# All weights stored in DRAM in the order of their tiles, one run of 4 or 8 KB per partition and load

## The chip, the cores and the metric

The kernel runs on one core of one Trainium2 chip. The metric is the device time of one execution, in microseconds (us). The core has a matrix engine (PE; its weight loads are listed apart as PEld), a vector engine (DVE), an activation engine (ACT), a general engine (POOL), a sync engine (SP, which here issues nearly all loads) and 16 DMA engines that carry the loads from DRAM into the core's memory of 128 partitions.

## The reference

Two transformer blocks follow each other on 256 tokens of width 1024. The first has two layers; each normalises and modulates the tokens, multiplies them with one wide projection matrix, runs attention, an mLSTM and a gated MLP side by side, and projects back:

```python
for l in range(DEPTH):                                   # block 1, DEPTH = 2
    mod_lat = silu_c @ w_ada[l] + b_ada[l]               # w_ada[l]: 1024 x 3072
    mod_ctx = silu_cc @ w_ada[l] + b_ada[l]
    x, ctx = _layer(x, ctx, mod_lat, mod_ctx, ...)       # w_in[l]: 1024 x 3344, w_out[l]: 1024 x 1024
x = _rms_norm(x, g_final)
for i in range(DEPTH):                                   # block 2
    mod = (ada_in @ w_ada_2[i] + b_ada_2[i]).reshape(b, 6, d)        # 1024 x 6144
    hm = rmsnorm(x, norm_mix[i]) * (1 + sc_m) + sh_m
    y = dilated_mixer(hm, a_w_in, a_w_out, ...) if i == 0 else forgetting_mixer(hm, b_w_in, b_w_out, ...)
    x = x + g_m * y
    hf = rmsnorm(x, norm_ffn[i]) * (1 + sc_f) + sh_f
    x = x + g_f * hierarchical_moe(hf, ..., w_gate[i], w_up[i], w_down[i])   # 16 experts
```

`a_w_in` is 1024 x 9216, `b_w_in` 1024 x 3088. `hierarchical_moe` gives every token two of 16 experts, each `silu(t @ w_gate) * (t @ w_up) @ w_down` with an inner width of 256. All values are float32, about 290 MB of weights in one execution.

## The kernel before, in words

Weights are read once, straight from DRAM, and used at once. Nearly every load goes into a tile called `raw`, 128 partitions x 4 x 512 float32 (1 MB); there are four of them, taken in turn, and a load into one waits until its last reader is done. SP issues the loads in program order, so an issue that waits holds back all later ones.

A projection takes the two halves (512 rows each) of a 1024 x 512 piece of its matrix as two `raw` tiles (`fetch`, L421). Row `k*128 + p` of a half lies in partition `p`, place `k`. ACT makes `wh`, an fp16 copy, DVE makes `wl`, the fp16 rest (L429), and PE multiplies `wh` and `wl` with the fp16 tokens `x`, and `wh` with their rest `y`. Where the 512 columns come from two places of the matrix, `fetch` issues one DMA for each place, and the rows of a DMA are as long as its piece of columns: 2 KB for 512 columns, 1 KB for 256, 64 bytes for the 16 gate columns.

The modulation is a matrix-vector product, straight in float32 on `raw` (`ps_ad<-raw,cz`). That of layer 0 is needed first of all and is done in four quarters (`ada_quarters`, L547): for each quarter two `raw` tiles, each of two DMAs of 512 KB with rows of 1 KB, one for the shift and one for the scale. After the second tile ACT copies the sum to `adasb`, PE transposes it, and DVE forms `mod` and `modA`. The tokens come in `xin` (four tiles, ctx and x); ACT squares each (`sq`), POOL makes the root `rs` in two steps, DVE scales `xin`; PE transposes it, and ACT and DVE form `nv` by `mod` and `modA`, then `x` and `y`, the two operands of the first projection, `kv` (272 columns). The other modulations load rows of 4 or 8 KB (L496).

In the MoE, two experts make a pair. `moe_gu` loads gate and up weights (L1930): every second pair into `raw`, 512 KB in rows of 4 KB for each DMA, the others into `x` tiles, 256 KB in rows of 2 KB. `moe_dn` loads `w_down` in rows of 8 KB, 1 MB in one run. After the first pairs stands a branch (`If`, L2114), for experts with more than 64 tokens; it isn't taken with these inputs, but every engine has to pass it.

The order of the instructions on each engine is set by a scheduler when the kernel is built, which estimates how long each instruction takes, the loads too.

Of the kernel before, what the change touches and what calls it, by code (L numbers as in the profile page):

```python
# [10 lines left out]
F32 = mybir.dt.float32  # L11
# [7 lines left out]
ds = bass.DynSlice  # L19
# [5 lines left out]
D = 1024  # L25
# [84 lines left out]
def quad(v):  # L110

    return np.ascontiguousarray(v.reshape(-1, 128, 4).transpose(1, 0, 2).reshape(128, -1))


# [45 lines left out]
class Stage:  # L160
# [251 lines left out]

    def fetch(self, segs, halves=range(2)):

        raws = []
        for hf in halves:
            raw = self.raw()
            o = 0
            for s in segs:
                n = s.shape[1]  # L420
                self.nc.sync.dma_start(raw[:, :, o:o + n],  # L421
                                       s.rearrange("(k p) n -> p k n", p=128)[:, 4 * hf:4 * hf + 4, :])
                o += n
            raws.append(raw[:, :, :o])
        return raws
# [20 lines left out]

    def load_w(self, segs):

        halves, raws = [], self.fetch(segs)
        self.convq.append((halves, self.conv_steps(raws, halves)))  # L450
        return halves
# [82 lines left out]
    def ada_quarters(self, gname, res):  # L534

        w, z, n = self.ap["w_ada"][0], self.cz, D // 4
        for r in range(2):
# [3 lines left out]
        for h in range(4):  # L541
            p = self.ps("ad")
            for k0 in (0, 4):
                raw = self.raw().rearrange("p a n -> p (a n)").rearrange("p (k j n) -> p k j n", k=4, j=2)
                for j in range(2):
                    src = w[k0 * 128:k0 * 128 + 512, j * D + h * n:j * D + h * n + n]
                    self.nc.sync.dma_start(raw[:, :, j], src.rearrange("(k p) n -> p k n", p=128))  # L547
                for k in range(4):
                    for j in range(2):
                        self.mm(p[32 * j:32 * j + 32, :n], z[:, k0 + k, :], raw[:, k, j], k0 + k == 0, k0 + k == 7,  # L550
                                tile_position=(0, 32 * j))
                if k0 == 0:
                    yield
            sb = self.w1("adasb")
            self.act(sb[:64], p[:64, :n], AF.Copy)
            q = self.ps("tr")
            for b in range(2):
                self.tr(q[:, b * 64:b * 64 + 64], sb[:64, b * 128:b * 128 + 128], 64)
            qv = q[:, :128].rearrange("p (b j r) -> p j b r", b=2, j=2)
            bias = self.P("bada1_0")[:, :16].rearrange("p (j k) -> p j k", j=2)  # L560
            c = slice(2 * h, 2 * h + 2)
            for r, (a, sh, sc) in reversed(list(enumerate(res))):
                self.tt(sc[:, c], qv[:, 1, :, r], bias[:, 1, c], OP.add)
                self.stt(a[:, c], sc[:, c], 1.0, self.P(f"{gname}_0")[:, c], OP.add, OP.mult)
                self.tt(sh[:, c], qv[:, 0, :, r], bias[:, 0, c], OP.add)
            yield
# [176 lines left out]
class Block1(Stage):  # L743
    def layer_w(self, l):

        w, wo = self.ap["w_in"][l], self.ap["w_out"][l]
        at = {"kv": ((1280, 1536), (3328, 3344)), "ckv": ((2304, 2816),), "cq": ((2048, 2304), (2816, 3072)),
              "z": ((3072, 3328), (512, 768)), "q": ((768, 1280),), "gmlp": ((0, 512),), "bz": ((1536, 2048),)}
        return [[w[:, a:b] for a, b in at[n]] for n in SEQ] + [[wo[:, 0:512]], [wo[:, 512:1024]]]

# [521 lines left out]
    def run(self):  # L1272
# [82 lines left out]
        def follow1(T, x):  # L1355
            r = self.rstd2(T)
            for n in range(2):
# [8 lines left out]

        w = self.ap["a_w_in"]
        self.W01 = self.layer(1, xT[1], W, (0, 1, 2, 3), loader(xd), gates1, follow1,
                              [[w[:, n * D:n * D + 512]] for n in range(2)])


class Block2(Block1):
# [220 lines left out]
    def dilated(self, xT):  # L1593
        nc = self.nc
        w = self.ap["a_w_in"]
# [3 lines left out]
        wo = [self.ap["a_w_out"][:, n * 512:(n + 1) * 512] for n in range(2)]  # L1599

        def load(n):
            if n < len(units):
                g, hf, k = units[n]
                c = (g * 3 + k) * D + hf * 512
                W[n] = self.load_w([w[:, c:c + 512]])
            else:
                W[n] = self.load_w([wo[n - len(units)]])

# [80 lines left out]
    def fox(self, xT, norm):  # L1689
        nc = self.nc  # L1690
        w = self.ap["b_w_in"]
        cols = [(k * D + hf * 512, k * D + hf * 512 + 512) for hf in range(2) for k in range(3)]
        W = {}
        wo = [self.ap["b_w_out"][:, n * 512:(n + 1) * 512] for n in range(2)]

        def load(n):
            if n < len(cols):
                W[n] = self.load_w([w[:, cols[n][0]:cols[n][1]]])
            else:
                W[n] = self.load_w([wo[n - len(cols)]])  # L1700
# [4 lines left out]
        nc.sync.dma_start(wr, w[:, 3072:3088].rearrange("(k p) n -> p k n", p=128))  # L1705
        W[0] = self.conv(self.fetch([w[:, cols[0][0]:cols[0][1]]]), 1)
        with self.tc.issue_after(self.tail[0]), self.tc.issue_after(self.tail[1]):
# [56 lines left out]
        for hf in range(2):  # L1764
# [8 lines left out]
            else:  # L1773
# [4 lines left out]
                for T in range(2):  # L1778
# [7 lines left out]
                                          U, lambda hf=hf, U=U: fin(hf, U), (s3[:, hs], NC)))  # L1786
        return [W[len(cols)], W[len(cols) + 1]]

# [129 lines left out]
    def moe_gu(self, i, P, part=range(8)):  # L1918
# [3 lines left out]
        for q in part:  # L1922
            a, k = divmod(2 * q, 8)
            if k % n:
                continue
            t = (self.x4(F32, (2, 512)) if P % 2 else self.raw()).rearrange("p a n -> p (a n)")
            t = t.rearrange("p (m j n) -> p m j n", m=2, j=n)
# [182 lines left out]
    def overflow(self, i, cnt, CAP):  # L2110
# [3 lines left out]
        with tc.If(rv > CAP):  # L2114
# [7 lines left out]
            with tc.For_i(0, 16, 1) as e:  # L2122
                raws = []
                for q in range(4):
                    t = self.wtile(("wh", "wl")[q % 2], (2, 512), F32)
                    for n, nm in enumerate(("w_gate", "w_up")):
                        nc.sync.dma_start(t[:, :, n * 256:n * 256 + 256],
                                          ap[nm][i, ds(e, 1)].rearrange("a (h p j) n -> p (a h) j n", h=2, j=4)[
                                              :, q // 2, q % 2 * 2:q % 2 * 2 + 2, :])
                    raws.append(t)  # L2130
                gc = self.small("gcol", 2)
                nc.vector.tensor_copy(gc[:, :, None], over[:, :, ds(e, 1)])
                hTs = []
                for T in range(2):
                    p = self.ps("tr")
                    for k in range(8):
                        self.mm(p, fT[:, k, T * 128:T * 128 + 128], raws[k // 2][:, k % 2], k == 0, k == 7)
                    t = self.w1("mt")
# [66 lines left out]
```

## Time and profile before

| | |
|---|---|
| median of 3 runs | 1310.13 us (1310.04 to 1313.8) |
| profiled execution | 1307.47 us, of which the span is 1305.5 us |
| PE busy | 1207.0 us, 92% of the span |
| DVE, ACT, POOL busy | 771.4, 628.1, 237.3 us |
| DMA | 292.36 MB, mean 224 GB/s; 114814 packets, 104724 of them under 8 KB |
| SP's hardware queue (q1) | 111972 packets, 60.8% of the 16 DMA engines' time |

The span is the time between the first and the last instruction of the profiled execution. A packet is one row of a transfer. The DMA share of a stretch can come out a little over 1, since packets of an engine overlap at their ends.

### The profile page before, as it was taken

To read this page: it belongs to the slowest core of one execution; us is meant where nothing else is said; L and a number is where in the kernel's file an instruction comes from. 1 tells how busy PE (TensorE), PEld (TensorE's weight loads), DVE (VectorE), ACT (ScalarE), POOL (GpSimd) and SP (SyncE) were. 2 spreads that over 40 slices of the span, in tenths; PEclk is the share of its full clock that TensorE was granted. 3 is DMA by queue.
4 is the path that set the end of the run, shared out by engine and by line. 5 is a ranking of instruction groups with operands and counts; after the bars stand their busy time and mean duration, and the time that the engine had idled before them with its cause. 6 is when DMAs were issued, how large, how long until landed. Compare 5 with 4: busy or idle time off the path is not lost. (4 is left out here: it accounts for less than half of the span.)

```text
span 1305.5 us, 21252 instructions
## 1 busy us (share of the span) xinstructions
PE 1207.0 (92%) x8064; PEld 574.9 (44%) x8064; DVE 771.4 (59%) x1787; ACT 628.1 (48%) x1373; POOL 237.3 (18%) x254
## 2 busy tenths in 40 slices
PE   6889999889999999899999999989997999889987
PEld 2434544444444544344545555445422445545432
DVE  3676645785568667866688767753213587663212
ACT  3535544443545545667677767433113656533111
POOL 1122000121230001251443234010001414010000
PEclk9999999999999999999999999989999899989998
DMA  9853456244384474598544545858898776618895
GB/s 322 284 173 135 163 186 214 94 161 148 135 273 157 139 265 154 185 324 307 167 163 161 194 162 210 299 219 300 342 353 313 269 292 228 227 37 324 329 354 198
DMA packets 114814, 292.36 MB, mean 224 GB/s; under 512 B 10890, under 2 KB 29450, under 8 KB 104724
## 3 DMA queue, kind: packets, MB, share of 16 engines
q1 hardware_dynamic: 111972, 281.57, 60.8%
q0 software_dynamic: 2736, 9.39, 2.3%
q8 instruction: 65, 1.06, 0.3%
q14 instruction: 41, 0.34, 0.1%
HBM read 288.80 MB, written 2.13 MB: 223 GB/s over the span
## 5 line engine op out<-in xcount | busy, mean ns | idle before, releaser
L264 PE MATMUL ps_mm<-wh,x 128*128 128x512 f16 (+1 forms) x1120 | 379.5, 378 | 4.6 <-DVE kn L251 2.0
L264 PEld LDWEIGHTS <-x 128*128 128x128 f16 (+1 forms) x2344 | 189.2, 98 | 245.9 <-issue 91.0
L264 PE MATMUL ps_mm<-wl,x 128*128 128x512 f16 (+1 forms) x736 | 276.0, 375 | 0.0
L429 DVE SCALAR_TENSOR_TENSOR wl<-raw,wh 128x1024 f16<-128x1024 f32 (+2 forms) x188 | 222.8, 1212 | 58.0 <-ACT wh L248 57.5
L248 ACT ACTIVATE wh<-raw 128x1024 f16<-128x1024 f32 (+2 forms) x188 | 182.8, 1015 | 62.5 <-PE ps_mm L264 56.0
L264 PE MATMUL ps_mm<-wh,y 128*128 128x512 f16 (+1 forms) x480 | 173.4, 373 | 0.4 <-DVE y L251 0.3
L264 PE MATMUL ps_ad<-raw,cz 128*32 128x512 f32 (+1 forms) x640 | 112.4, 569 | 11.7 <-DMA raw<-in_w_ada 11.7
L298 POOL TENSOR_SCALAR hss<-hss 128x8 f32<-128x8 f32 (+2 forms) x58 | 20.7, 357 | 444.6 <-DVE hss L697 425.7
L299 POOL TENSOR_TENSOR hr<-hss,nhalf 128x8 f32<-128x8 f32 (+2 forms) x58 | 90.5, 1561 | 4.8
L264 PEld LDWEIGHTS <-y 128*128 128x128 f16 x560 | 53.9, 99 | 60.3 <-issue 12.3
L259 DVE SCALAR_TENSOR_TENSOR oh<-ps_tr,ka,oh 128x512 f16<-128x512 f32 x32 | 24.0, 751 | 86.9 <-ACT oh L248 86.7
L248 ACT ACTIVATE e<-e,ka 128x128 f32<-128x128 f32 (+1 forms) x128 | 56.6, 443 | 24.8 <-DVE ka L1556 24.8
L268 PE MATMUL ps_tr<-consts,e 128*128 128x128 f32 x352 | 59.2, 280 | 1.7 <-ACT e L248 0.5
L264 PE MATMUL ps_mm<-wh,big 128*128 128x512 f16 x192 | 58.1, 379 | 0.2 <-DVE big L259 0.2
L268 PEld LDWEIGHTS ps_tr<-consts,e 128*128 128x128 f32 x352 | 40.8, 141 | 29.3 <-ACT e L248 6.0
L248 ACT ACTIVATE oh<-ps_tr,ka 128x512 f16<-128x512 f32 x32 | 22.0, 687 | 57.5 <-PE ps_tr L264 57.5
L251 DVE TENSOR_TENSOR e2l<-ps_tr,e2h 128x384 f16<-128x384 f32 x64 | 34.1, 553 | 23.4 <-ACT e2h L248 22.5
L248 ACT ACTIVATE e<-ps_s,mx 128x512 f32<-128x512 f32 (+1 forms) x48 | 29.1, 612 | 34.4 <-DVE mx L994 34.4
L251 DVE TENSOR_TENSOR el<-ps_tr,eh 128x512 f16<-128x512 f32 (+1 forms) x48 | 28.1, 597 | 27.2 <-ACT eh L248 27.0
L248 ACT ACTIVATE e2h<-ps_tr 128x384 f16<-128x384 f32 x64 | 30.0, 481 | 26.5 <-PE ps_o L264 14.5
L264 PEld LDWEIGHTS ps_ad<-raw,cz 128*32 128x32 f32 x640 | 21.0, 110 | 48.9 <-issue 27.1
L264 PEld LDWEIGHTS <-big 128*128 128x128 f16 x288 | 28.1, 98 | 32.4 <-DVE big L259 0.3
(377 smaller groups left out, 1988.1 us busy)
## 6 DMA issues: line engine op xcount, KB each, us to landing
raw<-in_w_ada SPq DMA_DIRECT2D x40, 1024.0 KB
raw<-in_a_w_in SPq DMA_DIRECT2D x36, 1024.0 KB
raw<-in_w_ada SPq DMA_DIRECT2D x64, 512.0 KB
raw<-in_w_in SPq DMA_DIRECT2D x16, 1024.0 KB
big<-in_w_down SPq DMA_DIRECT2D x16, 1024.0 KB
qk<-in_w_down SPq DMA_DIRECT2D x16, 1024.0 KB
x<-in_w_gate SPq DMA_DIRECT2D x64, 256.0 KB
x<-in_w_up SPq DMA_DIRECT2D x64, 256.0 KB
```

The costliest lines, as they stand in the source:

```text
L248: return self.nc.scalar.activation(out, in_, func, **kw)
L251: return self.nc.vector.tensor_tensor(out, a, b, op=op)
L259: return self.nc.vector.scalar_tensor_tensor(out, a, s, b, op0=op0, op1=op1)
L264: return self.nc.tensor.matmul(out, lhsT, rhs, start=start, stop=stop, **kw)
L268: return self.nc.tensor.transpose(out, in_, self.C("ident")[:n, :n])
L298: self.nc.gpsimd.tensor_scalar(in_, in_, eps, None, op0=OP.add)
L299: self.nc.gpsimd.tensor_tensor(out, in_, self.nhalf.to_broadcast(list(in_.shape)), op=OP.pow)
L429: (on or self.nc.vector).scalar_tensor_tensor(wl, raw, WS, wh, op0=OP.mult, op1=OP.subtract)
```

## The change

The host stores each weight matrix in the order in which the tiles want it: for each tile all its values of partition 0 (places `k` = 0 to 3 one behind the other), then those of partition 1, and so on. Each load is then one DMA with one run per partition: 8 KB for a `raw` tile, 4 KB for an `x` tile, 4352 bytes for `kv`, 512 bytes for the forget-gate columns `wfr` (before: 64 bytes). Where a tile was filled by two DMAs, one remains: SP has 369 rows in its order before, and 232 now. In a `raw` tile of the MoE the order of gate and up within a partition changes too, and the views follow. `w_down`, the other modulations (L496) and `bias` are as they were; so are the bytes, the tiles, their number, and the work of PE, ACT, DVE and POOL.

```diff
+def blocks(w):
+    return w.reshape(2, 4, 128, -1).transpose(0, 2, 1, 3).reshape(2, 128, -1)
+def weight_arrays(a):
+    w = {}
+    for l in range(2):
+        for n, cs in COLS.items():
+            w[f"w_{n}_{l}"] = blocks(np.concatenate([a["w_in"][l][:, c:d] for c, d in cs], 1))
...
+    v = a["w_ada"][0][:, :2 * D].reshape(2, 4, 128, 2, 4, D // 4)
+    w["w_ada_0"] = v.transpose(4, 0, 2, 1, 3, 5).reshape(4, 2, 128, -1)
+    v = np.stack([a["w_gate_2"], a["w_up_2"]], 2).reshape(2, 16, 2, 2, 128, 2, 2, 256)
+    w["w_gu"] = v.transpose(0, 1, 4, 3, 5, 2, 6, 7).reshape(2, 16, 128, 4096)
+    return w
...
-    def fetch(self, segs, halves=range(2)):
+    def fetch(self, src, halves=range(2)):
         raws = []
         for hf in halves:
-            raw = self.raw()
-            o = 0
-            for s in segs:
-                n = s.shape[1]
-                self.nc.sync.dma_start(raw[:, :, o:o + n],
-                                       s.rearrange("(k p) n -> p k n", p=128)[:, 4 * hf:4 * hf + 4, :])
-                o += n
-            raws.append(raw[:, :, :o])
+            n = src.shape[2]
+            raw = self.raw().rearrange("p k n -> p (k n)")[:, :n]
+            self.nc.sync.dma_start(raw, src[hf])
+            raws.append(raw.rearrange("p (k n) -> p k n", k=4))
         return raws
...
-                raw = self.raw().rearrange("p a n -> p (a n)").rearrange("p (k j n) -> p k j n", k=4, j=2)
-                for j in range(2):
-                    src = w[k0 * 128:k0 * 128 + 512, j * D + h * n:j * D + h * n + n]
-                    self.nc.sync.dma_start(raw[:, :, j], src.rearrange("(k p) n -> p k n", p=128))
+                raw = self.raw().rearrange("p a n -> p (a n)")
+                self.nc.sync.dma_start(raw, w[h, k0 // 4])
+                raw = raw.rearrange("p (k j n) -> p k j n", k=4, j=2)
...
-            for m, nm in enumerate(("w_gate", "w_up")):
-                src = self.ap[nm][i, 2 * P + a].rearrange("(h p j) n -> p h j n", h=2, j=4)
-                self.nc.sync.dma_start(t[:, m], src[:, k // 4, k % 4:k % 4 + n, :])
-            ws[a].extend(t[:, :, j] for j in range(n))
+            self.nc.sync.dma_start(t, self.ap["w_gu"][i, 2 * P + a][:, k * 512:(k + n) * 512])
+            t = t.rearrange("p (q m j n) -> p q m j n", q=n // 2, m=2, j=2)
+            ws[a].extend(t[:, j // 2, :, j % 2] for j in range(n))
```

The callers in block 1, in the two mixers of block 2 and in the branch of the MoE pass the new arrays in the same way.

Since the scheduler sees other loads, it also orders a few instructions otherwise, nearly all of them in the first 75 us. In the listings a row is a line of the kernel, the operation and what it writes and reads; a line number of the helpers is 34 higher after the change (L248 and L282 are the same line). POOL's order is the same in both.

On ACT, at the start of the program, before: the first of the four `xin` tiles is squared before the first `adasb`, three after it, and the second half of the `kv` weights is converted (`wh` with 2x272) after the second `adasb`.

```order
L248 ACTIVATE sq,ss<-xin 128x1024
L248 ACTIVATE adasb<-ps_ad 64x256
L248 ACTIVATE sq,ss<-xin 128x1024 x3
L248 ACTIVATE nv<-ps_tr,mod_103,modA_104 128x256
L248 ACTIVATE x_99<-nv 128x2x256
L248 ACTIVATE adasb<-ps_ad 64x256
L248 ACTIVATE wh<-raw 128x2x272 x2
L248 ACTIVATE nv<-ps_tr,mod_101,modA_102 128x256
```

And the same place after the change:

```order
L282 ACTIVATE sq,ss<-xin 128x1024 x2
L282 ACTIVATE adasb<-ps_ad 64x256
L282 ACTIVATE sq,ss<-xin 128x1024 x2
L282 ACTIVATE nv<-ps_tr,mod_103,modA_104 128x256
L282 ACTIVATE x_99<-nv 128x2x256
L282 ACTIVATE wh<-raw 128x2x272 x2
L282 ACTIVATE adasb<-ps_ad 64x256
L282 ACTIVATE nv<-ps_tr,mod_101,modA_102 128x256
```

One square has moved ahead of the first `adasb`, and the conversion ahead of the second. DVE's counterpart moves with it: the two `wl` rows (L429) of that half stand before the second group of `mod` and `modA` now, and after it before.

On SP, the loads of the first 60 us, before (`xin` are the tokens, `w_in` here the `kv` columns, then `q`):

```order
L547 DMA raw<-in_w_ada 128x4x256 x2
L421 DMA raw<-in_w_in 128x4x256
L421 DMA raw<-in_w_in 128x4x16
L1284 DMA xin<-in_ctx 128x1024
L547 DMA raw<-in_w_ada 128x4x256 x2
L1284 DMA xin<-in_ctx 128x1024
L1284 DMA xin<-in_x 128x1024 x2
L547 DMA raw<-in_w_ada 128x4x256 x4
L421 DMA raw<-in_w_in 128x4x256
L421 DMA raw<-in_w_in 128x4x16
L547 DMA raw<-in_w_ada 128x4x256 x8
L421 DMA raw<-in_w_in 128x4x512 x2
```

After the change:

```order
L575 DMA raw<-in_w_ada 128x2048
L453 DMA raw<-in_w_kv 128x1088
L1310 DMA xin<-in_ctx 128x1024
L575 DMA raw<-in_w_ada 128x2048
L1310 DMA xin<-in_ctx 128x1024
L1310 DMA xin<-in_x 128x1024 x2
L575 DMA raw<-in_w_ada 128x2048 x2
L453 DMA raw<-in_w_kv 128x1088
L575 DMA raw<-in_w_ada 128x2048 x4
L453 DMA raw<-in_w_q 128x2048 x2
```

The tiles are loaded in the same order; each pair of DMAs into one tile has become one.

## Rows read from the trace of the kernel before

**Rows 1.** Stretches: start, length, busy time (count) by engine, PE clock, DMA share, GB/s.

```profile
core 0: us, PE busy (x) PEld busy (x) DVE busy (x) ACT busy (x) POOL busy (x), PEclk, DMA share, GB/s
0.00:30.00 30.00, 18.05 (x98) 7.71 (x98) 9.91 (x34) 11.21 (x21) 5.09 (x15) 0.94 0.99 320
30.00:60.00 30.00, 23.69 (x167) 13.94 (x168) 16.85 (x44) 14.68 (x25) 1.25 (x4) 0.94 0.94 322
60.00:820.00 760.00, 726.04 (x5174) 354.41 (x5176) 527.81 (x1183) 432.25 (x953) 176.06 (x187) 1.00 0.54 185
820.00:1010.00 190.00, 172.98 (x1010) 74.05 (x1009) 71.28 (x193) 53.70 (x127) 10.82 (x9) 0.96 0.84 308
```

**Rows 2.** PE's waits, 0 to 62 us: total us, times, longest.

```profile
PE ps_ad L264 <- DMA raw<-in_w_ada: 8.1, 4, 5.8
PE ps_tr L268 <- DVE xin L255: 2.2, 1, 2.2
```

**Rows 3.** PE's waits, 62 to 820 us.

```profile
PE ps_ad L264 <- DMA raw<-in_w_ada: 3.6, 5, 1.9
```

**Rows 4.** PE's waits over the whole span, the other one for a load.

```profile
PE ps_mm L264 <- DMA raw<-in_w_up: 4.2, 2, 2.2
```

**Rows 5.** DMA from 3 to 36 us: packets, sizes, rate.

```profile
DMA packets 11085, 11.57 MB, mean 351 GB/s; under 512 B 1404, under 2 KB 10559, under 8 KB 11084
```

**Rows 6.** DMA from 17 to 23 us, nearly only rows of 1 KB.

```profile
DMA packets 2103, 2.09 MB, mean 348 GB/s; under 512 B 64, under 2 KB 2103, under 8 KB 2103
```

**Rows 7.** DMA from 38 to 41 us, nearly only rows of 2 KB.

```profile
DMA packets 564, 1.12 MB, mean 374 GB/s; under 512 B 16, under 2 KB 16, under 8 KB 564
```

**Rows 8.** DMA from 966 to 972.6 us, mostly rows of 4 KB.

```profile
DMA packets 756, 2.74 MB, mean 416 GB/s; under 512 B 87, under 2 KB 87, under 8 KB 755
```

**Rows 9.** DMA from 952.6 to 956.6 us, rows of 8 KB (`w_down`).

```profile
DMA packets 224, 1.70 MB, mean 424 GB/s; under 512 B 17, under 2 KB 17, under 8 KB 17
```

**Rows 10.** Instructions in time, start: start us, us, engine, line, operation [idle before <- releaser].

```profile
13.34 1.91 PE L264 MATMUL ps_ad<-raw,cz 128*32 128x256 f32 x14 [0.87 <-DMA raw<-in_w_ada]
15.29 0.38 ACT L248 ACTIVATE adasb<-ps_ad 64x256 f32<-64x256 f32 x1 [3.82 <-PE ps_ad L264]
15.56 1.04 ACT L248 ACTIVATE sq<-xin 128x1024 bf16<-128x1024 f32 x1
...
20.14 0.57 POOL L299 TENSOR_TENSOR rs<-ss,nhalf 128x1 f32<-128x1 f32 x1
...
21.41 0.54 DVE L256 TENSOR_SCALAR nv<-ps_tr,modA,mod 128x256 f32<-128x256 f32 x1
...
22.67 0.29 PE L264 MATMUL ps_mm<-wh,x 128*128 128x272 f16 x1
...
24.66 1.92 PE L264 MATMUL ps_ad<-raw,cz 128*32 128x256 f32 x16
26.62 0.38 ACT L248 ACTIVATE adasb<-ps_ad 64x256 f32<-64x256 f32 x1 [4.01 <-PE ps_ad L264]
26.90 1.19 ACT L248 ACTIVATE wh<-raw 128x544 f16<-128x544 f32 x2
...
28.00 1.36 DVE L429 SCALAR_TENSOR_TENSOR wl<-raw,wh 128x544 f16<-128x544 f32 x2
...
30.53 0.29 PE L264 MATMUL ps_s<-wh,x 128*128 128x272 f16 x1 [0.85 <-ACT x L248]
```

**Rows 11.** The same, 44 to 60 us.

```profile
44.63 1.92 PE L264 MATMUL ps_ad<-raw,cz 128*32 128x256 f32 x16
...
48.45 1.99 ACT L248 ACTIVATE wh<-raw 128x1024 f16<-128x1024 f32 x2
...
59.91 0.39 PE L264 MATMUL ps_mm<-wh,x 128*128 128x512 f16 x1 [2.00 <-DVE kn L251]
```

**Rows 12.** Stretch 52 to 56 us, columns as in rows 1.

```profile
52.00:56.00 4.00, 3.39 (x17) 2.31 (x18) 3.54 (x10) 2.10 (x3) 0.00 (x0) 0.57 1.09 342
```

**Rows 13.** The same as rows 10, behind the branch of the first MoE.

```profile
959.09 0.34 SPq L1930 DMA_DIRECT2D raw<-in_w_gate  x1
959.19 1.17 POOL L620 DMA_DIRECT2D gate<-gs  x2 [90.94 <-PEq L2114]
...
966.03 1.06 PE L264 MATMUL ps_mm<-raw,wh 128*64 128x512 f32 x2 [2.01 <-DMA raw<-in_w_up]
```

**Rows 14.** SP's waits, 948 to 960 us: total us, times, longest.

```profile
SPq L2114 <- SPq L2114: 8.1, 5, 2.5
```

**Rows 15.** Queues that fetch instructions, whole span: packets, MB, share of DMA time.

```profile
q8 instruction: 65, 1.06, 0.3%
q14 instruction: 41, 0.34, 0.1%
```

More of the change, by code (lines that the diff above doesn't have):

```diff
@@ L445, in conv, with load_w @@
         return halves
-    def load_w(self, segs):
-        halves, raws = [], self.fetch(segs)
+    def load_w(self, src):
+        halves, raws = [], self.fetch(src)
         self.convq.append((halves, self.conv_steps(raws, halves)))
@@ L744, in layer_w @@
     def layer_w(self, l):
[L746 to L749, printed above, removed]
+        return [self.ap[f"w_{n}_{l}"] for n in SEQ] + [self.ap[f"w_out_{l}"][n] for n in range(2)]
     def layer(self, l, xT, W, order, load_x, gates, follow, last, first=None):
@@ L1365, in follow1 @@
             self.done.add(("x", T))
-        w = self.ap["a_w_in"]
         self.W01 = self.layer(1, xT[1], W, (0, 1, 2, 3), loader(xd), gates1, follow1,
-                              [[w[:, n * D:n * D + 512]] for n in range(2)])
+                              [self.ap["a_w_in"][n] for n in range(2)])
 class Block2(Block1):
@@ L1598, in dilated @@
         W = {}
-        wo = [self.ap["a_w_out"][:, n * 512:(n + 1) * 512] for n in range(2)]
+        wo = [self.ap["a_w_out"][n] for n in range(2)]
         def load(n):
             if n < len(units):
-                g, hf, k = units[n]
-                c = (g * 3 + k) * D + hf * 512
-                W[n] = self.load_w([w[:, c:c + 512]])
+                W[n] = self.load_w(self.ap["a_w_in"][n])
             else:
-                W[n] = self.load_w([wo[n - len(units)]])
+                W[n] = self.load_w(wo[n - len(units)])
         def merge(hf, g, Us):
@@ L1690, in fox @@
         nc = self.nc
-        w = self.ap["b_w_in"]
-        cols = [(k * D + hf * 512, k * D + hf * 512 + 512) for hf in range(2) for k in range(3)]
         W = {}
-        wo = [self.ap["b_w_out"][:, n * 512:(n + 1) * 512] for n in range(2)]
+        units = [self.ap["b_w_in"][n] for n in range(6)] + [self.ap["b_w_out"][n] for n in range(2)]
         def load(n):
[L1697 to L1700, printed above, removed]
+            W[n] = self.load_w(units[n])
         lf = self.keep("lf", 2, 16)
@@ L1704, in fox @@
         wr = self.w1("wfr", (8, 16))
-        nc.sync.dma_start(wr, w[:, 3072:3088].rearrange("(k p) n -> p k n", p=128))
-        W[0] = self.conv(self.fetch([w[:, cols[0][0]:cols[0][1]]]), 1)
+        nc.sync.dma_start(wr.rearrange("p k n -> p (k n)"), self.ap["b_w_f"])
+        W[0] = self.conv(self.fetch(units[0]), 1)
         with self.tc.issue_after(self.tail[0]), self.tc.issue_after(self.tail[1]):
@@ L2188 @@
         "bias2": dilated_bias(a["rel_bias_2"]),
[L2189 to L2191 removed]
+        "w_down": a["w_down_2"], **weight_arrays(a),
         "w_ada_2": a["w_ada_2"], "b_ada_2": a["b_ada_2"],
     }
[L2194 removed]
+    for n in ("w_ada", "b_ada", "g_final"):
         arrs[n] = a[n]
```

34 lines of the change are left out of this document (19 added, 15 removed).

## The prediction

> **What bounds the kernel now.** I read the stretches first, then PE's list of waits, then the DMA rates, and only then single instructions in the places that these three point to. The stretches [rows 1] show two kernels in one. From 60 to 820 us PE is busy 726 of 760 us and the DMA engines are on average half idle: a faster load changes nothing there except where PE stands still for one. In the first 60 us it is the other way: the DMA share is 0.99 and 0.94, and PE works 18.05 and 23.69 of 30 us each. In the first MoE (820 to 1010 us) both are loaded, PE 172.98 of 190 us and DMA 0.84. The list of waits then says what loads cost PE directly: 8.1 us in the first 62 us [rows 2], 3.6 us up to 820 us [rows 3], and 4.2 us in the two MoEs, once in each [rows 4]. (A wait of 2.2 us for `xin` stands behind the load too, through the chain below [rows 2].) The waits for loads are 15.9 us, the most that faster loads can give by these waits alone; more can only come where a late load delayed ACT or DVE first.
>
> The rates tell how much faster a row gets when it is longer. Where the queue is full, rows of 1 KB moved at 348 GB/s [rows 6], 2 KB at 374 [rows 7], 4 KB at 416 [rows 8], 8 KB at 424 [rows 9]; the last is `w_down`, which before the change already is what all loads become, a tile of 1 MB in one run. So 1 KB to 8 KB takes 18% off a transfer (1 - 348/424), 2 KB 12%, 4 KB 2%. From 3 to 36 us the mean is 351 GB/s, and 10559 of 11085 packets are under 2 KB [rows 5]: the stretch that hangs most on loads has the shortest rows.
>
> The Trainium skill ("DMA: Bandwidth & Descriptors", Specifications) says otherwise: 512 B is enough for line rate, and about 358 GB/s is what the DRAM gives one core. By that, rows of 1 KB at 348 have nothing left to gain. The trace disagrees with it, with 424 GB/s at 8 KB [rows 9]; it is weighed below.
>
> **The change part by part.** *The start.* The first product of the modulation needs its second `raw` tile, on which PE waits until 13.34 us [rows 10]. Ahead of and with it SP has asked for two tiles of 1 MB, 0.56 MB of `kv` weights, and 0.5 MB of tokens, 3.27 MB (in units of 10^6 bytes) with the small constants. At the mean of the stretch, 351 [rows 5], that takes 9.3 us, at 424 7.7 us. The tokens have rows of 4 KB already, so I take 1.4 us: the tile comes at about 11.9 instead of 13.3 us, and `adasb` at 13.9 instead of 15.29.
>
> What follows is a chain of small operations on ACT, POOL and DVE. The last three tiles of tokens are squared from 15.56 on, behind `adasb`; POOL's last root starts at 20.14, DVE's `nv` at 21.41, PE's first `kv` matmul at 22.67 [rows 10]. The new order squares the second tile ahead of `adasb`. Its tokens lie in the queue just behind the tile of the modulation, 0.52 MB or 1.2 us later, at 13.1 us; so this square runs from 13.1 to 14.3, 2.3 us earlier than at 15.56 to 16.6, and `adasb` waits for it by some 0.4 us, which the chain of roots hides. POOL's three roots follow the second square at the same pace, since its order and work are the same. I take 2.1 us: the first `kv` matmul at 20.6 instead of 22.67.
>
> The next step is the second quarter (`ps_ad` at 24.66, `adasb` at 26.62). Behind it ACT converts the second half of the `kv` weights (1.19 us from 26.90) and DVE too (1.36 us from 28.00), before they get to `nv` and `x`; only then PE goes on, at 30.53 [rows 10]. In the new order both conversions stand ahead of `adasb`. ACT and DVE are free then, while PE multiplies (20.6 to 24.5 us), if the load is in: the bytes ahead of it and its own are 7.5 MB, about 20.5 us at 424. So their time leaves the path. Not all of the 1.36 us: PE transposes and ACT works on the other half of `nv` meanwhile, so I take 0.8 us. If the load came later than 24.5 us, `adasb` would wait behind it, and these 0.8 us would become a loss of about 1.2; the 4 us between make that unlikely. Together 2.9 us by 30.53.
>
> From there PE is nearly without a gap up to the last quarter at 44.63 [rows 11] and doesn't wait for a load, and a load can't run further ahead than the four tiles, which PE itself frees. What the loads save here stays hidden. At 48.45 ACT converts two pieces in a row (1.99 us) that the new order takes apart, one of them ahead of `nv`, in a gap of ACT: 0.3 us, by 0 to 0.5. So the start gives 2.9 + 0.3 = 3.2 us, and PE's matmul of 59.91 would start at 56.7.
>
> Its bounds: nothing below 1.4 us, the tile's own, unless a rival below takes it back. Above, if all 33 us of [rows 5] were a wait for data, 11.57 MB would take 27.3 instead of 33 us: 5.7 us.
>
> *The middle, 62 to 820 us.* The rows there are 2 KB or 1 KB for projections, and the modulations (unchanged) lie behind them in the same queue. PE waits 3.6 us in five places, 1.9 us in one of them [rows 3]. There the transfer ahead is one tile of the projection (1.05 MB); 348 to 424 takes it from 3.0 to 2.5 us, and one issue less saves about 0.3 us (0.34 us for one at [rows 13]). I take 0.8 us for all five, 0 to 3.6. Nothing else is on the path: PE is the bound.
>
> *The two MoEs.* Rows of 2 KB become 4 KB and of 4 KB 8 KB. PE waits for them only behind the branch: SP gets to the loads at 959.09, PE starts 6.94 us later, having waited 2.01 us [rows 13]. The first tile is two DMAs (gate, up), one now, so its second half is asked for about 0.35 us earlier; and two transfers that POOL issues at the same time share the DMA engines. I take 0.35 us for each of the two MoEs, 0.7 us (0 to 4.2, rows 4). Its cover: none, PE runs on at once.
>
> *Nothing* for the 137 rows fewer on SP: its issues wait for buffers, not for SP. *Nothing* for `wfr` (512 bytes instead of 64 in each row, 64 KB).
>
> The sum is 3.2 + 0.8 + 0.7 = 4.7 us, off the profiled 1307.47 us. I take the same difference from the median of the runs, 1310.13: **1305.4 us**. About 0.3% (3.9 us) is what a measurement of this kernel can tell from no change, so it would count as faster below 1306.2.
>
> **The rivals.** *Hidden or given back.* The start is a chain of waits between five engines, of which the load is one; if the roots or `adasb` set it, or PE idles later instead, 1.4 us or less remain of 3.2, and the rest may give nothing: 1308.5 to 1310.5. It would also go so if the DMA engines gain nothing by longer rows, or still split them: with the rates unchanged, only the reordering of 0.8 to 1.5 us is left, 1309. For it speaks that PE is 92% busy; against it the four rates [rows 6 to 9]. That the rates stay is what the rule of the Trainium skill cited above would make of this change.
>
> *The start hangs on data throughout.* Then it gives 5.7 us [rows 5], with 1.5 us from the rest 7.2. From 52 to 56 us the clock granted to PE was 0.57 [rows 12], so PE's 3.39 us there would take about 2 at full clock; if this stretch goes too, 1.4 more. 1301.5 to 1303. For it speaks the share of 0.99; against it, that PE runs from 30 to 46 us without waiting for a load.
>
> *Slower: instructions come later.* The engines' instructions are fetched over the same DMA engines, 65 and 41 packets [rows 15]. A fetch that stands behind one row on its engine waits for it: 47 ns for 1 KB (348 GB/s over 16 engines), 88 ns for 2 KB, 309 ns for 8 KB. So each can come 0.22 to 0.26 us later, 106 of them 23 to 28 us if all were waited for. It needs 8.6 us (4.7 to undo and 3.9 beyond), which is some 36 of 106 on the path: 1314 to 1320. Against it: fetching shows as a wait at the branch, where SP waits 8.1 us in five pieces [rows 14], and there the queue is full of `w_down`'s 8 KB rows already, so this doesn't get worse. Elsewhere I see no such wait.
>
> **How the numbers follow.** My forecast (1304 to 1307.5) has a chance of 0.45, hidden or given back 0.27, data throughout 0.20, slower 0.08. Of the first, about four fifths lie below 1306.2: faster 0.20 + 0.36 = 0.56. Same is 0.09 + 0.27 = 0.36, slower 0.08. The range runs from 1300.5 (data throughout, and more of the middle's 3.6 us) to 1311.0 (nothing gained, and the spread of the runs); it leaves out the slower case and the tails.
>
> **What would show it.** From 3 to 36 us a rate above 400 GB/s instead of 351, and only the token tiles' rows under 8 KB. The second tile of the modulation lands at about 11.9 us, the first `kv` matmul starts at 20.6, the matmul of 30.53 at 27.7, that of 59.91 at 56.7. PE's wait for `in_w_ada` falls from 11.7 us (rows 2 and 3) by some 2 to 3, that in the MoEs from 4.2 to about 3.5. I am wrong if the rates don't rise; if they do and 59.91 moves by less than 1.5 us, the start is no chain of loads; if it moves by 3 and the whole doesn't, the gain is lost further on.

## The result

| | before | changed |
|---|---|---|
| median of 5 runs | 1313.11 us (1310.04 to 1313.92) | 1299.76 us (1296.04 to 1302.97) |
| ratio | | 0.9896, 95% interval 0.9874 to 0.9919 |
| profiled execution | 1307.47 us, span 1305.5 | 1301.36 us, span 1299.2 |

The changed kernel is faster by 1.0%, about 13.4 us by the medians, where 4.7 us were forecast and 1300.5 us was the low end of the range. A second set of runs gave 0.9893 (0.9871 to 0.9916). The two profiled executions lie only 6.3 us apart in span. One execution is a poor yardstick here: the timed runs of before scatter from 1302.13 us (granted clock 0.981 over the run) to 1320.5 us (0.966), since the stretches at half clock differ from one execution to the next. One more run of before, 1837 us long at a granted clock of 0.617, is left out of every comparison. So the sums below are made by medians of many runs, and the traces say where.

The page of the changed kernel, its head, PE, and the loads:

```profile
span 1299.2 us, 21044 instructions
PE 1207.5 (93%) x8064; PEld 574.7 (44%) x8064; DVE 772.2 (59%) x1787; ACT 628.1 (48%) x1373; POOL 235.2 (18%) x254
DMA packets 51133, 292.34 MB, mean 225 GB/s; under 512 B 5962, under 2 KB 6218, under 8 KB 24660
q1 hardware_dynamic: 48292, 281.56, 58.7%
```

The bytes are the same and the packets less than half; SP's queue needs 58.7% of the DMA engines' time instead of 60.8%. So the change did what it says, and PE's own work (1207.5 us, 1207.0 before) did not change. PE's waits for loads in the whole span, all in one line (total us, times, longest), which answers to rows 2 to 4:

```profile
PE ps_ad L298 <- DMA raw<-in_w_ada: 13.8, 7, 6.7
```

The wait for `in_w_ada` has not fallen by 2 to 3 us but risen, from 11.7 to 13.8 us (12.4 in a second execution). Part of it is that PE now begins with a tile only when the whole tile has landed: its first product starts at 6.71 us, and before, with half a tile, at 5.82:

```profile
5.82 1.03 PE L264 MATMUL ps_ad<-raw,cz 128*32 128x256 f32 x2 [5.82 <-DMA raw<-in_w_ada]
```

The wait for the MoE's weights, 4.2 us in [rows 4], is not 3.5 as forecast but gone. At the start, DMA from 3 to 36 us (as [rows 5]) and instructions in time (as [rows 10, 11]):

```profile
DMA packets 2171, 12.71 MB, mean 385 GB/s; under 512 B 240, under 2 KB 245, under 8 KB 1013
```

```profile
6.71 3.63 PE L298 MATMUL ps_ad<-raw,cz 128*32 128x256 f32 x16 [6.71 <-DMA raw<-in_w_ada]
...
11.76 3.63 PE L298 MATMUL ps_ad<-raw,cz 128*32 128x256 f32 x16 [1.42 <-DMA raw<-in_w_ada]
...
15.43 0.38 ACT L282 ACTIVATE adasb<-ps_ad 64x256 f32<-64x256 f32 x1 [1.26 <-PE ps_ad L298]
...
21.28 0.29 PE L298 MATMUL ps_mm<-wh,x 128*128 128x272 f16 x1 [1.20 <-ACT x L282]
...
29.08 0.29 PE L298 MATMUL ps_s<-wh,x 128*128 128x272 f16 x1
...
55.19 0.39 PE L298 MATMUL ps_mm<-wh,x 128*128 128x512 f16 x1 [1.74 <-DVE kn L285]
```

The second tile is there at 11.76 us (13.3 before, 11.9 forecast), the first `kv` matmul at 21.28 (22.67 before, 20.6 forecast), the matmul of 59.91 at 55.19 (56.7 forecast). So far the gain is 4.7 us. Behind the first MoE's branch (as [rows 13, 14]):

```profile
949.60 0.80 SPq L1952 DMA_DIRECT2D qk<-in_w_down  x2
...
953.01 1.88 SPq L1944 DMA_DIRECT2D raw<-in_w_gu  x4
...
964.58 1.02 PE L298 MATMUL ps_mm<-raw,wh 128*64 128x512 f32 x2
```

And SP's waits there:

```profile
SPq L2129 <- SPq L2129: 1.3, 2, 0.8
```

SP issues the last loads ahead of the branch at 949.6, as before (948.88), but the first behind it at 953.0 instead of 959.09; its waits at the branch are 1.3 us instead of 8.1 [rows 14], and in the second MoE 1.6 instead of 8.4. PE then finds its weights in place. This is what the prediction didn't have, and the experiments are mostly about it.

### The profile page after: what moved, and what is told of

Read it like the earlier page. It is cut to its first block, busy times and chain, and to the rows that moved or that the text cites. A ratio compares the mean times of both kernels' runs of the same rounds, so it can differ in the third digit from the quotient of the medians.

```text
span 1299.2 us, 21044 instructions
## 1 busy us (share of the span) xinstructions
PE 1207.5 (93%) x8064; PEld 574.7 (44%) x8064; DVE 772.2 (59%) x1787; ACT 628.1 (48%) x1373; POOL 235.2 (18%) x254
## 3 DMA queue, kind: packets, MB, share of 16 engines
q1 hardware_dynamic: 48292, 281.56, 58.7%
## 5 line engine op out<-in xcount | busy, mean ns | idle before, releaser
L282 ACT ACTIVATE wh<-raw 128x1024 f16<-128x1024 f32 (+2 forms) x188 | 183.1, 1015 | 62.6 <-PE ps_mm L298 56.5
L298 PE MATMUL ps_ad<-raw,cz 128*32 128x512 f32 (+1 forms) x640 | 112.3, 577 | 13.9 <-DMA raw<-in_w_ada 13.8
L298 PEld LDWEIGHTS <-y 128*128 128x128 f16 x560 | 54.0, 100 | 60.6 <-issue 13.8
L282 ACT ACTIVATE e<-e,ka 128x128 f32<-128x128 f32 (+1 forms) x128 | 56.6, 443 | 24.5 <-DVE ka L1581 24.5
L282 ACT ACTIVATE oh<-ps_tr,ka 128x512 f16<-128x512 f32 x32 | 22.0, 687 | 54.5 <-PE ps_tr L298 54.5
L282 ACT ACTIVATE e<-ps_s,mx 128x512 f32<-128x512 f32 (+1 forms) x48 | 29.2, 612 | 34.4 <-DVE mx L1020 34.4
L282 ACT ACTIVATE e2h<-ps_tr 128x384 f16<-128x384 f32 x64 | 30.0, 481 | 26.5 <-PE ps_o L298 14.5
```

The lines of the kernel that those rows point to most:

```text
L282: return self.nc.scalar.activation(out, in_, func, **kw)
L298: return self.nc.tensor.matmul(out, lhsT, rhs, start=start, stop=stop, **kw)
```

## The experiments

The prices are ratios to runs of the kernel before on the same chip.

**Which part pays?** Four kernels take the kernel before and one part of the change each. The diffs are cut to their main lines. *e1_gu*, only the MoE's gate and up loads:

```diff
-            for m, nm in enumerate(("w_gate", "w_up")):
-                self.nc.sync.dma_start(t[:, m], src[:, k // 4, k % 4:k % 4 + n, :])
+            self.nc.sync.dma_start(t, self.ap["w_gu"][i, 2 * P + a][:, k * 512:(k + n) * 512])
```

> The kernel before, with only the MoE's gate and up loads changed (one DMA a tile, rows of 4 and 8 KB); the loop in the branch still has its eight loads. In the changed kernel SP came to the four raw loads behind the branch at 953.0 us instead of 959.1, and each MoE gave about 3.5 us. Theory A (the emptier queue: fewer and larger DMAs let SP finish the x loads by 941 us, and its instructions at the branch are then fetched past an emptier queue): SP waits under 2 us at the branch, PE doesn't wait for in_w_gu, 6 to 8 us faster than before. Theory B (the shorter loop: SP's own code in the branch is half as long): SP still waits 7 to 9 us at the branch, PE still 1.5 to 2 us for in_w_gu in each MoE, 0 to 2 us faster. Theory C (the rate: only the loads behind the branch arrive faster): SP as before at the branch, PE's wait down from 2.0 to about 1.6, under 1.5 us faster.

*e2_body*, only the loop over experts in the branch that isn't taken:

```diff
                 for q in range(4):
-                    for n, nm in enumerate(("w_gate", "w_up")):
-                        nc.sync.dma_start(t[:, :, n * 256:n * 256 + 256], ap[nm][i, ds(e, 1)]...)
+                    nc.sync.dma_start(t, ap["w_gu"][i, ds(e, 1)]...[:, q * 1024:q * 1024 + 1024])
```

> The kernel before, with only the loop in the branch that isn't taken changed (four loads instead of eight for gate and up). No instruction that is executed differs, and no load. Theory A (emptier queue) and C (rate): same time within 1 us, SP waits about 8 us at the branch. Theory B (shorter code): SP waits under 2 us there, PE no longer waits for in_w_up, 6 to 8 us faster.

*e3_ada0*, only the first modulation's tiles:

```diff
-                for j in range(2):
-                    self.nc.sync.dma_start(raw[:, :, j], src.rearrange("(k p) n -> p k n", p=128))
+                self.nc.sync.dma_start(raw, w[h, k0 // 4])
```

> The kernel before, with only the first modulation's eight tiles changed (rows of 8 KB instead of 1 KB, eight DMAs instead of sixteen). If the start's gain comes from the tile on which the first product waits, as predicted: the rate between 3 and 30 us rises above 380 GB/s, the matmul that started at 59.9 us starts at 55.5 to 57.5, the whole is 2 to 4 us faster. If the projection's loads carry it: under 1.5 us.

*e4_fetch*, only the projections' loads:

```diff
-            for s in segs:
-                self.nc.sync.dma_start(raw[:, :, o:o + n], s.rearrange(...)[:, 4 * hf:4 * hf + 4, :])
+            self.nc.sync.dma_start(raw, src[hf])
```

> The kernel before, with only the projections' loads changed (w_in, w_out, a_w_in, a_w_out, b_w_in, b_w_out and the forget gate's columns: one DMA a tile, rows of 8 KB or 4352 bytes instead of 2 KB, 1 KB and 64 bytes). Predicted: 0.8 us from the middle, and at the start at most 1 us from the kv columns' 64-byte rows: 0 to 2 us faster, the matmul of 59.9 us at 59 or later. If the projections' loads carry the start's gain, it moves by 2 us or more. PE's waits for in_w_ada between 62 and 820 us were 3.6 us before and 4.3 in the changed kernel, so I expect no gain from the middle.

| | ratio | interval | SP's waits at the two branches, us | PE's wait for gate and up, us |
|---|---|---|---|---|
| e1_gu | 1.0025 | 1.0006 to 1.0044 | 7.9, 9.4 | 5.1 |
| e2_body | 0.9952 | 0.9924 to 0.9980 | 3.0, 3.6 | 0.2 |
| e3_ada0 | 0.9977 | 0.9957 to 0.9997 | 7.8, 8.5 | 2.2 |
| e4_fetch | 1.0007 | 0.9985 to 1.0029 | 8.1, 8.4 | 3.1 |

The kernel in which no load that is executed differs, e2_body, gains most, 6.3 us. Theories A (emptier queue) and C (rate) fall. B has the right place and nearly the right times; but its reason, the length of the code, is not the cause, and the expectation errs in saying that no executed instruction differs: SP has two rows fewer to run at the branch, as shown below. e3_ada0 gains 3.0 us, as expected, with 375 GB/s from 3 to 30 us, just under the 380 expected; e4_fetch gains nothing, though its matmul of 59.91 comes at 58.24, earlier than the 59 expected. SP's and PE's waits in e2_body, in the first MoE and in the whole span:

```profile
SPq L2114 <- SPq L2114: 3.0, 2, 2.3
```

```profile
PE ps_mm L264 <- DMA x<-in_w_up: 0.2, 1, 0.2
```

Row for row these are [rows 14] with 8.1 and [rows 4] with 4.2. e1_gu comes out a little slower than before. In its second MoE PE waits 4.25 us for a tile that is now one load of 1 MB (0.9 us in the first); SP's waits there, and PE's start behind them:

```profile
SPq L2112 <- SPq L2112: 9.4, 3, 5.2
```

```profile
1252.87 2.00 SPq L1927 DMA_DIRECT2D raw<-in_w_gu  x4
...
1260.42 1.97 PE L264 MATMUL ps_mm<-raw,wh 128*64 128x512 f32 x2 [4.25 <-DMA raw<-in_w_gu]
```

**The changed kernel with one part taken back.** *f1_after* is the changed kernel once more.

> The changed kernel once more, for a second execution in the profile and for its time beside the runs below. The time should be 0.985 to 0.993 of before. If the start's gain is the chain of loads, the matmul that started at 59.9 us before starts between 55 and 57 again, whatever the clock does. If the half-clock stretches of the first 60 us, which the first execution of the changed kernel didn't have, are what the change takes away, there are none here either.

*f2_oldbody* has the loop of before, with its eight loads (the reverse of e2_body's edit).

> The changed kernel, with only the loop in the branch that isn't taken as it was before (eight loads for gate and up instead of four). Nothing that is executed differs. Theory B (shorter code of SP in the branch; the runs so far are for it): SP waits 7 to 10 us at the branch again instead of 1.3 and 1.6, PE waits 2 to 4 us for in_w_gu in each MoE, and of the changed kernel's gain 5 to 9 us are gone: 0.993 to 0.999 of before. Rival (the fewer, larger loads do it and the loop was of use only beside small ones): as the changed kernel, within 2 us.

*f4_no_gu* has the MoE's loads of before (the reverse of e1_gu's edit).

> The changed kernel, with only the MoE's gate and up loads as before (two DMAs a tile, rows of 2 and 4 KB); the loop in the branch is the short one. If the MoE's gain comes from the short loop alone: PE's waits for in_w_up near 0, as the changed kernel within 2 us. If longer rows and fewer DMAs in the MoE have a part of their own: 3 us or more slower than the changed kernel.

*f3_before* is the kernel before once more.

> The kernel before once more, one look: a second execution in the profile. The profiled execution of before took 1307.5 us, less than the median of its timed runs, about 1312. I expect a span of 1306 to 1314 us, with the same waits for loads (11 to 12 us for in_w_ada, 3 to 5 for in_w_up, 7 to 9 us of SP at each branch) and more time at half clock than the 57 us of the first execution, in the stretches that other runs show there.

f1_after 0.9893 (0.9871 to 0.9916), f4_no_gu 0.9902 (0.9880 to 0.9924), f2_oldbody 0.9964 (0.9945 to 0.9984). Two thirds of the gain hang on the loop: with the old one the median is 1308.31 us, with the new one 1298.46. SP's waits in f2_oldbody, first MoE, and PE's in the whole span:

```profile
SPq L2129 <- SPq L2129: 7.2, 4, 3.5
```

```profile
PE ps_mm L298 <- DMA raw<-in_w_gu: 4.7, 2, 4.5
```

In f4_no_gu, where the loads of the MoE are the short ones, PE has no wait for them (SP's are 2.7 and 3.0 us). So beside the short loop the rows and the number of these loads don't show in the time. f1_after has half clock from 17.4 to 24.2 us (0.57 over 17 to 25 us), so the change doesn't free the first 60 us of it.

f3_before had a span of 1308.5 us and nearly the waits of the first execution: 11.8 us of PE for `in_w_ada`, 8.2 and 8.3 us of SP, but only 2.5 us of PE for `in_w_up`, where 3 to 5 were expected. Against f1_after's 1293.9 us this pair is 14.6 us apart; the medians are 15.0 apart. By PE's matmuls, in order, the changed kernel is ahead by 3.8 us at the matmul of 59.91 (60.33 and 56.51), by 5.8 at 869.0 (863.2), by 6.8 at 965.1, before the branch, by 10.7 at 994.9, behind it, by 11.2 at 1253.4, at the second branch, and by 14.6 at the end. Of the 2 us between 60 and 870, 1.4 are a stretch at half clock that f3_before has at 553.7 us and f1_after doesn't. The step at the branch is larger than PE's wait: PE goes on at half clock after it (970.2 to 973.6 us). The first execution of before has such a stretch there too; that one, and the same place in the changed kernel (columns as in rows 1):

```profile
966.90:970.30 3.40, 3.40 (x10) 1.50 (x10) 0.00 (x0) 0.38 (x1) 0.00 (x0) 0.50 1.02 414
```

```profile
964.50:968.00 3.50, 3.50 (x16) 1.36 (x15) 0.80 (x2) 1.07 (x2) 0.00 (x0) 1.00 0.99 360
```

In 3.4 us PE starts 10 matmuls at the granted clock of 0.50 (the lower of its two levels, 1.2 GHz), and in 3.5 us 16 at 1.00. So of the step of 3.9 us 2.1 are f3_before's wait for the load, and most of the other 1.8 the slower work behind it. Half clock follows PE's wait at one of the two branches in six of the nine traces in which SP waits 7 us or more at each, so it comes often, not always.

**Is it SP's code, and how much of it?** Three kernels change only the loop of the kernel before, and one that of the changed kernel. *g1_six* loads two of the loop's four tiles by one DMA (six loads):

```diff
+                    if q < 2:
+                        nc.sync.dma_start(t..., ap["w_gj"][i, ds(e, 1)]...[:, q * 1024:q * 1024 + 1024])
```

> The kernel before, with six loads for gate and up in the loop of the branch that isn't taken (two of the four tiles by one DMA), between the eight of before and the four of the change. Nothing that is executed differs. SP waited 8.1 to 8.5 us at each branch with eight and 3.0 and 3.6 with four. If its wait grows with the length of the code: 5 to 7 us, PE waits 0 to 1.5 us for in_w_up in each MoE, 2 to 4 us faster than before. If it is a matter of whether one more piece of code must be fetched: about 8 or about 3 us, and the time like before or like four loads.

*g2_pool* issues the eight loads from POOL:

```diff
-                        nc.sync.dma_start(t[:, :, n * 256:n * 256 + 256], ...)
+                        nc.gpsimd.dma_start(t[:, :, n * 256:n * 256 + 256], ...)
```

> The kernel before, with the loop's eight loads of gate and up issued by POOL instead of SP: the same loop, the same arrays and shapes, but SP's code in it is 16 rows shorter and POOL's longer. If SP's code in the branch is what costs: SP waits under 3 us at the branch, PE doesn't wait for in_w_up, 5 to 8 us faster than before, as with four loads. If the loop's new array or PE's new view of the tiles did it: as before, SP at 8 us.

*g3_sixteen* halves each load:

```diff
+                        for b in range(2):
+                            nc.sync.dma_start(t[:, b, n * 256:n * 256 + 256], ...)
```

> The kernel before, with sixteen loads for gate and up in the loop instead of eight. Nothing that is executed differs. If SP's wait at the branch grows with the code: 14 to 18 us, PE's wait for in_w_up 7 to 10 us in each MoE instead of 2, 10 to 18 us slower than before. If the code of eight loads is already beyond what is at hand, and a jump costs the same from there on: 8 to 9 us of SP, the time of before.

*g4_after_pool* is the changed kernel with all the loop's loads on POOL (`nc.gpsimd.dma_start` for the four of gate and up and the two of `w_down`).

> The changed kernel, with all loads of the loop issued by POOL: SP has no code in the branch and passes no branch at all. SP waited 1.3 to 2.1 us there and PE didn't wait for in_w_gu, so I expect the time of the changed kernel within 2 us. If it is faster by 3 us or more, even the short code of SP still held the loads back. POOL's longer way through the branch delays its two gate loads, which nobody waited for so far: if they come on the path, 1 to 4 us slower.

| SP's gate and up loads in the loop | kernel | SP's semaphore rows at each branch | SP's waits at the two branches, us | ratio |
|---|---|---|---|---|
| 16 | g3_sixteen | 8 | 8.0, 8.5 | 1.0009 (0.9993 to 1.0025) |
| 8 | f3_before | 8 | 8.2, 8.3 | 1 |
| 6 | g1_six | 8 | 7.8, 8.5 | 0.9998 (0.9978 to 1.0018) |
| 4 | e2_body | 6 | 3.0, 3.6 | 0.9952 (0.9924 to 0.9980) |
| 0 | g2_pool | 2 | 0.2, 0.9 | 0.9958 (0.9938 to 0.9978) |

It is a step and no slope: with 6, 8 and 16 loads the way past the branch costs the same 8 us, with 4 some 3, with none nearly nothing. The first MoE's rows of g3_sixteen and g2_pool:

```profile
SPq L2114 <- SPq L2114: 8.0, 4, 2.6
```

```profile
SPq L2114 <- SPq L2114: 0.2, 1, 0.2
```

g2_pool has the old arrays, the old shapes and the old loop, and gains as e2_body does; so what counts is what SP has in the loop, not the new array.

**What SP waits for.** The column of semaphore rows gives the reason, and it is not the length of the code. A semaphore is a counter that a load raises when it lands. SP's rows under the branch's own line in the first MoE of g3_sixteen, before, e2_body and g2_pool, in this order (count, ns, first and last start):

```profile
L2114 SPq EVENT_SEMAPHORE  x8: 17/17/17, 957.4 to 963.4; - x8
L2114 SPq EVENT_SEMAPHORE  x8: 17/17/17, 952.5 to 958.7; - x8
L2114 SPq EVENT_SEMAPHORE  x6: 17/17/17, 958.0 to 959.0; - x6
L2114 SPq EVENT_SEMAPHORE  x2: 17/17/17, 955.4 to 955.5; - x2
```

In this program SP's loads take eight semaphores in turn. Where the loop is skipped, SP runs one row for each semaphore that its loads in the loop would have raised: the row waits until SP's earlier load on that semaphore has landed, and then raises it in the loop's place. In before the rows start at 952.45, 953.12, 955.59 and 958.06 us; by the trace's records of the semaphores the loads had landed at 952.43, 953.10, 955.58 and 958.04. The other four rows find their loads landed and are done by 958.69. The third and the fourth of these loads are the two of `w_down`, 1 MB each, issued at 948.88 and 949.31, right ahead of the branch. So SP's 8.1 us are a wait for its own loads, before it may issue the next ones.

That explains the step. With the two loads of `w_down` in the loop, 6, 8 and 16 loads of gate and up use all eight semaphores. With 4 they use six, the next in turn, and the two left out are those of the two `w_down` loads under way: e2_body's first two rows start at 957.99 and 958.65, for landings at 957.97 and 958.64 of loads ahead of these, and the others follow at once. With none they use two, whose loads have landed. The other traces agree at both branches: all 98 rows that start more than 0.5 us after the row before them do so within 0.03 us of the landing on their semaphore. The changed kernel has six rows like e2_body, and waits less (1.3 and 1.6 us; f4_no_gu with the small loads 2.7 and 3.0), since its fewer, larger `x` loads were issued earlier: the last 10.4 us ahead of the branch (940.54 and 950.99), in e2_body 2.3 us (953.28 and 955.62).

What remains for a fetch of code is little: in g4_after_pool, whose SP still has the branch to pass, against the expectation, but no semaphore row, 0.8 us lie between the branch (953.92) and SP's next load (954.73). Nor does the number of fetched packets follow the wait: 65 and 41 on the two instruction queues in the whole span of before [rows 15], 65 and 40 in the changed kernel, 65 and 42 in g2_pool.

What the wait costs PE can be read between the same matmuls of all traces, counted in order: from the 6256th to the 6481st, around the first branch, and from the 7861st to the last, around the second. Seven traces with eight rows and the small loads take 122.6 to 127.1 us for both together (mean 125.0), two with eight rows and the large loads 126.1 and 127.4. Three with six or two rows and the small loads take 117.7 to 118.2 (mean 118.0), four with six or no rows and the large loads 117.3 to 117.7 (mean 117.5). So the eight rows cost about 7.0 us, and the larger loads bring about 0.5 us more beside few rows, and nothing beside eight.

g4_after_pool gave 0.9921 (0.9899 to 0.9943), no better than the changed kernel, and at the two branches its trace takes as long as f1_after's (117.5 and 117.3 us): the 1.3 to 2.1 us that remained held nobody up.

**Do the parts add up?** *h1_start* takes e3_ada0 and e4_fetch together, *h2_moe* e1_gu and e2_body.

> The kernel before, with the first modulation's tiles and all projections' loads changed; the MoE's loads and the loop in the branch are as before. If the prediction of the loads' gain at the start (3.2 us, and 0.8 in the middle) holds: 3 to 5 us faster, the matmul of 59.9 us at 55 to 57.5. If the 0.36% that remained beside the old loop came from the MoE's loads: under 1.5 us. SP at the branch as before, about 8 us.

> The kernel before, with the MoE's gate and up loads and the loop in the branch changed; the start and all projections as before. The loop alone gave 0.48% (6.3 us), the changed kernel has 1.07% (14 us). If the parts add up: 8 to 10 us faster, SP under 3 us at the branch, no wait of PE for in_w_gu, the matmul of 59.9 us where it was. If the loads matter nothing beside the short loop: 5 to 7 us.

h1_start 0.9964 (0.9944 to 0.9983), h2_moe 0.9928 (0.9906 to 0.9949). Together -0.36% and -0.72%, or 4.7 and 9.5 us, which is the changed kernel's 1.07%. The 9.5 us are some 3 more than e2_body's 6.3, as if the larger loads had a part of their own beside the short loop; f4_no_gu and the 0.5 us between the matmuls above speak against it, and the intervals of the two runs overlap. In h1_start the matmul of 59.91 starts at 55.37 us, and SP and PE wait at the branch as before (8.0 and 9.3 us; 4.9); in h2_moe it starts at 61.65, no earlier than before, and SP waits 0.8 and 1.5 us. The two parts of h1_start gave 0.23% and nothing by themselves, less than together, at the edge of what the intervals tell apart; at the matmul of 59.91 they give 57.29 and 58.24.

## Why the prediction was wrong

**The rates: right in kind, too high.** Rows of 8 KB are faster: 385 GB/s from 3 to 36 us instead of 351 [rows 5], in f1_after 373. Forecast was above 400. That is what the queue moves while it is full, 406 from 3 to 20 us and 421 from 20 to 30. From 30 to 36 us it is 268 at a DMA share of 0.82: the loads have run ahead, and SP waits for PE to free the tiles (18.9 us between 3 and 40 us, 9.8 before). Besides the tokens' rows the 4352-byte rows of `kv` are under 8 KB too, which the prediction left out. The Trainium skill's limit of about 358 GB/s, a stack's bandwidth split between two cores ("DMA: Bandwidth & Descriptors", Specifications), doesn't hold here, where one core runs: the trace disagrees, with 385 over 33 us.

**The start: near in size, in other shares.** 3.2 us were forecast. The matmul of 59.91 moved by 4.7 us in the first pair of traces and 3.8 in the second, and h1_start's runs give 4.7. Over all traces it starts at 59.75 to 62.95 us with the start of before (eight traces, mean 61.2) and at 55.19 to 57.85 with both parts of the changed start (six, mean 56.6). Of the first pair's 4.7 us, 1.4 are won by the first `kv` matmul, not 2.1. The second tile landed at 11.76, as forecast, but `adasb` came at 15.43, later than before, since the sixteen products took 3.63 us instead of the 1.91 us of the last fourteen before [rows 10]. That is the slow pace which the very first tile's products have in most traces (3.62 us for the last fourteen in before, 2.92 to 3.63 over all). In f1_after they took 1.92, and `adasb` came at 14.46; why the pace differs I can't say, for the granted clock in the rows is 1.00 both times.

From the second quarter's product to the last quarter's the changed start needs 18.87 us (23.27 to 42.14) and that of before 19.97 (24.66 to 44.63), alike to 0.02 us in every trace with either start. These 1.1 us fit the conversions that left the path, put at 0.8 (PE's wait of 0.85 us for ACT at 30.53 [rows 10] is gone); they show later than forecast, since the matmul of 30.53 moved by 1.45 us and not by 2.9. From the last quarter's product to the matmul of 59.91 before took 15.28 us, and the six traces with the changed start 13.04 to 13.06. g1_six has the start of before, and no half clock there:

```profile
46.54 1.92 PE L264 MATMUL ps_ad<-raw,cz 128*32 128x256 f32 x16
...
60.91 0.39 PE L264 MATMUL ps_mm<-wh,x 128*128 128x512 f16 x1 [2.00 <-DVE kn L251]
```

It takes 14.37 us. So 0.9 of the 2.2 us are the half-clock stretch of [rows 12], only a rival's extra in the prediction (1.4 us), and 1.3 are left, which fits the new order that the prediction put at 0.3 us there. PE's waits for ACT's and DVE's operands of the `ps_s` products tell where, in before and in the changed kernel:

```profile
51.02 0.29 PE L264 MATMUL ps_s<-wh,x 128*128 128x272 f16 x1 [1.17 <-ACT x L248]
...
52.61 0.41 PE L264 MATMUL ps_s<-wh,y 128*128 128x272 f16 x1 [0.96 <-DVE y L251]
```

```profile
48.03 0.29 PE L298 MATMUL ps_s<-wh,x 128*128 128x272 f16 x1 [0.18 <-ACT x L282]
...
48.99 0.29 PE L298 MATMUL ps_s<-wh,y 128*128 128x272 f16 x1 [0.32 <-DVE y L285]
```

**The middle: nothing, not 0.8 us.** PE's waits for `in_w_ada` between 62 and 820 us were 3.6 and 3.8 us in two executions of before, and 4.3 and 2.3 in two of the changed kernel; over all traces they average 3.8 us with the projections' loads as before (nine) and 3.7 with the new ones (seven). The step that failed is the one that took 0.5 us off the tile in front and 0.3 off an issue; nothing of it is seen in the waits.

**The MoEs: 0.7 us forecast, 7.5 (traces) to 9.5 (h2_moe's runs) measured.** This is the term that put the time outside the range. The step took SP's arrival at the loads (959.09) as given and asked only how fast they would land. The text read the wait at the branch [rows 14] as the fetching of instructions, which "doesn't get worse" with longer rows. It is SP's wait for its own earlier loads, on eight semaphores, and it does get better when the loop uses only six of them: 1.3 us instead of 8.1. The sentence that put SP's fewer rows at nothing, "its issues wait for buffers, not for SP", is where the gain was thrown away. It counts the loads that are issued; among the rows that went were loads in a loop that is skipped, and for those SP has to wait as well. The bound was in the text too: 4.2 us for the waits. Even it was too low, since PE often runs on at half clock after such a wait (up to 1.8 us more at the first branch), and since in runs with the old loop and the larger tiles the wait is up to 4.5 us.

**The rivals.** "Slower: instructions come later" looked at the right place, the branch, but for the wrong cause and with the wrong sign. "Data throughout" (5.7 us at the start) was close for h1_start's 4.7 but not for its reason, since PE's wait for `in_w_ada` rose. "Hidden or given back" is right for the middle alone.

## What to carry to other kernels

Look at what stands right ahead of a late load on the engine that issues it: a wait there, even one that the profile puts down to the issuing engine itself, sets when the load starts, and the load's own length matters less. Loads in a branch that is never taken aren't free in a program built like this one: the engine that would issue them waits, on its way past, for earlier loads that share their semaphores. Keep them off the queue that has to issue loads right behind the branch, or keep them few, so that the loads under way just ahead of it aren't waited for. Look for semaphore rows in the trace under the branch's own line. And when PE stands idle for a load, count what its lower clock can cost behind the wait as well.

## What the runs showed of the hardware

- Passing a branch that isn't taken cost SP about 8 us when its code in the branch held 6, 8 or 16 loads (beside two of `w_down`), 0.8 to 3.6 us with 4, and 0.2 to 0.9 with none. The waits are for loads of SP's own to land; without a semaphore row the way past took 0.8 us in all. DVE's wait for PE at the first branch was 7.4 us before and after the change.
- While the queue was full, rows of mostly 8 KB moved 406 to 421 GB/s from 3 to 30 us, where rows of mostly 1 KB had moved 341 to 358.
- Executions of one kernel differ by up to 1.4% (1302.13 to 1320.5 us for before). Two traces of before had about 55 and 73 us at half clock (mean granted clock 0.979 and 0.972).
